# Attention outputs with values as the stationary operand, two heads side by side in the columns

## The chip, the core and the metric

One core of a Trainium2 chip runs the whole program. The metric is device time in microseconds (us). The core's engines are TensorE (PE: matmuls and transposes; PEld in the profile: its weight loads), VectorE (DVE), ScalarE (ACT), GpSimd (POOL) and SyncE (SP, which issues the DMAs). A matmul reads a stationary operand, loaded into the 128 x 128 array first, and streams a moving operand through it.

## The reference

A decoder trunk of two layers over 256 tokens of width 1024, in float32. In each layer the input is RMS-normed and multiplied by one large matrix whose columns feed four token mixers of 4 heads x 64 and four gates. All mixers end in softmax attention:

```python
# A: top-64 keys by an indexer, one shared key/value head
# B: causal over all 256 keys, 4 key/value heads
# C: compressed keys + selected blocks + window, each with sigmoid gates
# D: window 128, 2 key/value heads, learned sinks
p = masked_softmax(q @ k.T * 64 ** -0.5, ok)      # e / max(sum(e), 1e-30)
o = p @ v                                         # (256 tokens, 4 heads, 64)
y = concat(o over heads)                          # (256, 256)
m = sum over mixers of sigmoid(gate) * (y @ w_branch)
x = x + m @ w_out
x = x + down(conv_silu_gate(up(rms_norm(x))))
```

With 256 tokens mixer C runs its "selected" and its "window" attention over all causal keys, each with its own keys and values, and adds both to the compressed one, each part scaled by a gate for each token and head.

## The kernel before

Tokens lie in two blocks of 128 (`NT = 2`), with the token on the partition, or transposed, with the feature on the partition and 256 token columns. Every weight matrix is loaded in chunks (`loads`, line 440), copied to a rounded part by ScalarE (`split_hi`, 460) and subtracted by VectorE to a rest (`split_lo`, 470); three products (rounded activations x rounded weights, rest x rounded, rounded x rest) make up one float32 product (`macs`, 490). These are the records `mm<-hi,ahi`, `mm<-hi,alo`, `mm<-lo,ahi` of the profile (and `ahi,hi` and so on in the feed-forward part).

The order of instructions is worked out while the program is built. Each piece of work is a stream, a generator that yields `(engine, needs, rings)` ahead of what it emits; `Flow.run` (140) always emits the step that can start first by estimated clocks, priorities breaking ties. A step that asks for engine "AV" goes to ScalarE or VectorE (line 149):

```python
eng = "ACT" if max(self.clock["ACT"], t) <= max(self.clock["DVE"], t) + 100 else "DVE"
```

`Eng.cost` (180) holds the estimates. Every engine then executes its instructions in that order. `main` (1246) is the stream of the large products: the projections of mixers A, B, D, C, then for each mixer its gate chunks and `branch_out` (1299), which multiplies y with `w_branch`. The mixers are streams beside it that start as their projections are out.

`attend` (632) is called ten times a layer: once for each block of 128 queries (t = 0, 1) in A, B, D, and twice in C (`nsa`, lines 999 to 1015). A call with t = 0 sees 128 keys, one with t = 1 sees 256. It makes scores over the 64 partitions of a head (line 646; the even heads in the lower half of the partitions, the odd ones in the upper half), masks them and takes the maximum (`attend_max`, 729), exponentiates each head on ScalarE with the sum as a by-product (653), spawns `recip` (708: maximum with 1e-30, reciprocal, in C times the gate), transposes the unnormalized exponentials `Sx` on TensorE (675, 681), copies them out of PSUM as `pT` (`evac_tr`, 739), and multiplies:

```python
for h in range(H):
    for b in range(t + 1):
        te = P.matmul(op[:, h, :], pT[:, h, b, :], vfn(h, b), start=b == 0, stop=b == t)
```

Here `pT[:, h, b, :]` (128 keys x 128 queries) is loaded as the stationary operand and 64 columns of values move. The result has the query on the partition. VectorE multiplies it with the reciprocal `rd` on the way out of PSUM (696 or 700), and in C adds it to y in a second step (703). When a mixer's y (128 x 2 x 256) is complete, `y_T` (579) calls `rows_T` (564): four transposes on TensorE (570), a rounding copy by ScalarE (573) and a subtraction by VectorE (575) give the two parts that `branch_out` needs.

`nsa_cmp` (1056) is C's attention over 15 compressed keys; it handles four heads in one product per block of queries (line 1092) and normalizes on the way out (1096).

Buffers are rings: PSUM banks for large products (`mm_r`, four), scores (`sc_r`, two) and transposes and small products (`tr_r`, two); two buffers for `Sx` (`sx_r`), two for `pT` (`pt_r`), four sets of small statistics (`sm_r`), one temporary `ot_r` (1017).

In the profile a float32 product stands as two load-and-matmul records, a transpose as one. `tr<-slotQ,f` and `tr<-kvA,f` are the products of probabilities (`f`) and values (`slotQ` for B, C, D, `kvA` for A), `tr<-cst,slotQ` the transposes of y, `sc<-qk` the scores. A shape such as "128*128 128x64" means 128 rows by 128 columns loaded and 128 x 64 moved. All calls go through one helper, so every line is given as L212.

Of the kernel before, what the change touches and what calls it, by code (L numbers as in the profile page):

```python
# [32 lines left out]
def constants():  # L33
    """What depends on shapes alone: identity, causal masks, rotary tables, a selection of rows."""
    c = np.zeros((128, C_END), np.float32)
    i = np.arange(128)
    c[:, C_ID:C_TRI] = np.eye(128)
    j = np.arange(256)
    diff = (128 + i)[:, None] - j[None, :]
    c[:, C_TRI:C_DM] = np.where(diff >= 0, 0.0, NEG)  # L40
    c[:, C_DM:C_CM] = np.where((diff >= 0) & (diff < 128), 0.0, NEG)
    t = (np.arange(2)[None, :, None] * 128 + i[:, None, None])
    ok = (np.arange(NCMP) * 16 + 31)[None, None, :] <= t
    c[:, C_CM:C_OK] = np.where(ok, 0.0, NEG).reshape(128, 30)
    c[:, C_OK:C_COS] = ok.reshape(128, 30)
    for dim, a, b in ((64, C_COS, C_SIN), (32, C_COSI, C_SINI)):
        inv = np.float32(10000.0) ** (-np.arange(0, dim, 2, dtype=np.float32) / np.float32(dim))
        ang = np.arange(S, dtype=np.float32)[:, None] * inv[None, :].astype(np.float32)
        co, si = np.cos(ang), np.sin(ang)
        cd = np.concatenate([co, co], 1).reshape(2, 128, dim).transpose(1, 0, 2)  # L50
        sd = np.concatenate([si, -si], 1).reshape(2, 128, dim).transpose(1, 0, 2)
        c[:, a:a + 2 * dim] = cd.reshape(128, 2 * dim)
        c[:, b:b + 2 * dim] = sd.reshape(128, 2 * dim)
    for h in range(H):
        c[32 * h:32 * h + 32, C_BLK + h] = 1.0
    for cc in range(2):
        for n in range(NCMP):
            for v in range(2):
                c[30 * v + 15 * cc + n, C_SEL + 15 * cc + n] = 1.0
    return c  # L60


# [8 lines left out]
class Ring:  # L71
    """slots that streams take and give back"""
# [14 lines left out]
class Flow:  # L87
    """A step of a stream is what it emits after `yield (engine, needs, rings)`: instructions of that
    one engine. The step that can start first is emitted next, so each engine meets its
    instructions in the order in which their operands are expected."""  # L90
# [23 lines left out]
    def moved(self, byts):  # L114
        """a transfer: issued in turn, eight under way at most, one after the other through the engines"""
        s = max(self.clock["SP"], self.need, self.ends[-8] if len(self.ends) >= 8 else 0.0)
        self.emitted = True
        self.clock["SP"] = s + 475
        self.wire = max(self.wire, s + 1100) + byts / 360.0
        self.ends.append(self.wire + 900)  # L120
        return self.ends[-1]
# [52 lines left out]
class Eng:  # L174
    """an engine of nc whose calls also advance the expected clock"""

    def __init__(self, flow, name, real):
        self.flow, self.name, self.real = flow, name, real

    def cost(self, m, a, k):  # L180
        aps = [v for v in list(a) + list(k.values()) if hasattr(v, "shape")]
        n = max(free_size(v) for v in aps)
        psum = any(v.tensor.name[:2] in ("mm", "sc", "tr") and v.tensor.name[2].isdigit() for v in aps)
        if self.name == "PE":
            n = free_size(a[0])
            if m == "transpose":
                c = 0.835 * n
            else:
                c = 0.417 * n + 2 if a[1].dtype == F32R else 1.67 * max(n, free_size(a[1])) + 2
            return c * (1 if self.flow.clock["PE"] > 6700 else 2)  # L190
        ptrs = sum(hasattr(k.get(q), "shape") for q in ("scale", "bias", "accum_out", "scalar"))
        if self.name == "ACT":
            return (52 if psum else 98) + 0.833 * n + 93 * ptrs
        if self.name == "DVE":
            if m == "tensor_copy" and not psum:
                return 62 + 0.54 * n
            if m == "scalar_tensor_tensor":
                ptrs = hasattr(a[2], "shape")
            elif m == "tensor_tensor_reduce":
                ptrs -= 1  # L200
            else:
                ptrs = 0
            return 68 + 1.04 * n + 62 * ptrs
        if self.name == "POOL":
            return 310 + 165 * n if k.get("op") == ALU.pow else 120 + 2.14 * n
        return 50
# [22 lines left out]
def trunk(ctx: ExitStack, tc: tile.TileContext, a, out):  # L229
# [72 lines left out]
    def warm():  # L302
        """the tensor engine's clock rises after some microseconds of work: keeps it busy until the first products"""
# [19 lines left out]
    def rsqrt(o, scale):  # L323
        """after a step of DVE: o = (o * scale + eps) ** -0.5"""
# [165 lines left out]
    def macs(ch, pieces, ps, get, futs, k0, first, last, ends=None):  # L490
        """rows: ps[t] += act(k0..) @ chunk"""
# [72 lines left out]
    def rows_T(src, needs, dst, k0, fut, scale=1.0):  # L564
        """256 columns of rows into two tiles of transposed halves"""
# [13 lines left out]
    def y_T(y, yf, yT, f):  # L579
        yT += yield "PE", [yf], [y_r]  # L580
        yield from rows_T(y, [yf], yT[0], 0, f)

# [7 lines left out]
    def head_rstd(src, h, d, r, rt, needs):  # L590
        """r (128, NT * h) = rsqrt of the mean square of src (128, NT, h, d)"""
# [8 lines left out]
    def rope(o, src, h, d, c, s, rt, needs, dup=1):  # L600
        """src (128, NT, h, d) -> o (128, NT, h, dup, d)"""
# [18 lines left out]
    def T_pairs(o, src, n, needs):  # L620
        """rows (128, NT, n * 128) -> o (128, n, 256)"""
# [10 lines left out]
    def attend(t, qT, kblk, kT, vfn, scl, mask, y, needs, sink=None, fin=None, gate=None):  # L632
# [30 lines left out]
        fl.spawn(recip(t2, den, rd, gate, rdf), 8)  # L663
        tes = []
        pTt = None
        for g in range(t + 1):
            if g == 0:
                pTt, tb = yield "PE", [te], [pt_r, tr_r]
                pT = pTt.rearrange("p (h b q) -> p h b q", h=H, b=2)
            else:  # L670
                tb, = yield "PE", [], [tr_r]
# [14 lines left out]
        sx_r.give(sxt, tq)  # L686
        ob, = yield "PE", tes, [tr_r]
        op = ob[:, :256].rearrange("p (h d) -> p h d", h=H)
        for h in range(H):
            for b in range(t + 1):  # L690
                te = P.matmul(op[:, h, :], pT[:, h, b, :], vfn(h, b), start=b == 0, stop=b == t)
        pt_r.give(pTt, te)
        rdb = rd[:, :, None].to_broadcast([128, H, DH])
        if gate is None:
            yield "DVE", [te, rdf], []
            te = V.tensor_tensor(heads(y)[:, t], op, rdb, op=ALU.mult)
            tr_r.give(ob, te)
        else:
            otmp, = yield "DVE", [te, rdf], [ot_r]
            te = V.tensor_tensor(otmp, op, rdb, op=ALU.mult)  # L700
            tr_r.give(ob, te)
            yield "DVE", [te], []
            te = V.tensor_tensor(heads(y)[:, t], heads(y)[:, t], otmp, op=ALU.add)
            ot_r.give(otmp, te)
        sm_r.give(sm, te)
# [12 lines left out]
    class _Pair(Fut):  # L718
        """known once both entries of a list are"""
# [24 lines left out]
    def qk_done(slot, futs, t_fut, n):  # L744
        """gives the slot back and notes y once n units are through"""
# [271 lines left out]
    ot_r = Ring([junk[:, :256].rearrange("p (h d) -> p h d", h=H)])  # L1017

    class Hidden:
        """what the products with c_cmp_w1 take from and give to the mixer"""  # L1020
# [4 lines left out]
    def hidden(i, ch, hid):  # L1025
        """pairs of chunks side by side: the blocks on the diagonal are wanted"""
# [29 lines left out]
    def nsa_cmp(qT, needs, tvb, cgv, y, y0):  # L1056
        """two heads a product over queries and compressed keys, four over probabilities and compressed values"""
# [25 lines left out]
        fl.spawn(cmp_den(tp_, Pv, crd, cgv, crd_f := Fut()), 12)  # L1083
        pTt, tb = yield "PE", [tp_], [pt_r, tr_r]
# [6 lines left out]
        for t in range(NT):  # L1091
            te = P.matmul(tb[:, t * 256:t * 256 + 256], pTt[:, t * 128:t * 128 + 128], vbd.rearrange("p h d -> p (h d)"),
                          start=True, stop=True)
        pt_r.give(pTt, te)
        yield "DVE", [te, crd_f], []
        te = V.tensor_tensor(heads(y), tb.rearrange("p (t h d) -> p t h d", t=NT, h=H),
                             crd[:, :, :, None].to_broadcast([128, NT, H, DH]), op=ALU.mult)
# [62 lines left out]
    def taps(col, ci_, u, a, z, t, f, fa):  # L1160
        """one channel block: the last tap, with the bias, and the first one into z; the middle one into a"""
# [10 lines left out]
    def conv(col, u, a, z, c0, t):  # L1172
        """two channel blocks through the causal convolution"""
# [8 lines left out]
    def conv_pair(col, ps, rg, g, t, rbf, cs, tmp, gf, gT, f):  # L1182
        """a bank of two channel blocks; the gates also through their silu"""
# [21 lines left out]
    def gated(tmp, needs, cs, gT, f):  # L1205
        """the gates times the values, in two parts"""
# [11 lines left out]
    def conv_first(col, bank, te, rbf, g, tmp, gf, gT, f):  # L1218
        """the first pair, with a bank for each block"""
# [26 lines left out]
    def main():  # L1246
        def open_layer(l, xf):
            """what the products of a layer start from"""
# [11 lines left out]
        for l in range(DEPTH):  # L1260
# [20 lines left out]
            # first group: both chunks over the first half of k, then over the second  # L1281
# [165 lines left out]
```

## Time and profile before

| | us |
|---|---|
| median of 3 runs | 881.3 |
| the runs | 881.3, 881.18, 885.47 |
| span of the profiled execution, first to last instruction | 884.2 |
| the profiled execution's own time | not listed; of the three runs only 885.47 is longer than the span |
| TensorE busy | 877.4 |
| VectorE busy | 675.7 |
| ScalarE busy | 535.8 |

A busy time is the union of an engine's records. Matmul records overlap, as one starts before the one ahead has left the array; what a matmul costs TensorE is read from the distance of starts in the timeline. A timeline row merges neighbours of the same form on an engine: start, time from the first start to the last end, count.

### The profile page before, as it was taken

How to read it: one execution, taken by the hardware profiler on the slowest of the kernel's cores; microseconds unless marked ns; L12 is line 12 of the kernel's file. 1: busy time of each engine (PE TensorE's matmuls, PEld its weight loads, DVE VectorE, ACT ScalarE, POOL GpSimd, SP SyncE). 2: the span in 40 equal slices, each digit the busy share in tenths (PEclk: the TensorE clock that was granted, in tenths of full speed). 3: DMA queues.
4: the chain of work that ended last, by engine and by line, in shares of the span. 5: the costliest groups of instructions: out<-in, count | busy, mean ns of one | idle time of the engine just before them, and what ended most of it. 6: DMA issues, size and time to landing. Idle time of an engine off the chain costs nothing.

```text
span 884.2 us, 14084 instructions
## 1 busy us (share of the span) xinstructions
PE 877.4 (99%) x5435; PEld 770.9 (87%) x5435; DVE 675.7 (76%) x1301; ACT 535.8 (61%) x907; POOL 35.1 (4%) x30
## 2 busy tenths in 40 slices
PE   8999999999999999999999999999999999999998
PEld 8979787788889999998898888887888899999886
DVE  4779988956767999984557998978476599899652
ACT  5555575644557887864455466646454598888531
POOL 0111002000000000000000111010000000000000
PEclk9999999999999999999999999999999999999999
DMA  7727454144645756555555264452446556556560
GB/s 264 237 87 238 143 187 148 48 143 147 215 162 168 229 166 220 184 183 190 160 181 167 78 211 143 143 171 74 161 167 216 165 164 218 191 192 192 173 230 24
DMA packets 103412, 149.89 MB, mean 170 GB/s; under 512 B 4072, under 2 KB 62258, under 8 KB 103346
## 3 DMA queue, kind: packets, MB, share of 16 engines
q1 hardware_dynamic: 103346, 149.01, 52.0%
q8 instruction: 42, 0.69, 0.3%
q14 instruction: 24, 0.20, 0.1%
HBM read 147.95 MB, written 1.05 MB: 169 GB/s over the span
## 4 chain that ended last, share of the span: by engine, by line
PE 98%; DMA 1%; ACT 0%; SPq 0%; DVE 0%; issue 0%; DVEq 0%
PE mm L212 82%; PE tr L212 8%; PE sc L212 8%; DMA rn<-in_norm_g_dram 1%; ACT f L212 0%; ACT L212 0%; SPq L239 0%; ACT hi L212 0%; DVE x L212 0%; DVEq L1443 0%
## 5 line engine op out<-in xcount | busy, mean ns | idle before, releaser
L212 DVE TENSOR_TENSOR lo<-raw,hi 128x1024 fp32r<-128x1024 f32 (+3 forms) x288 | 337.7, 1179 | 119.9 <-ACT hi L212 112.7
L212 ACT ACTIVATE hi<-raw 128x1024 fp32r<-128x1024 f32 (+3 forms) x288 | 291.5, 1023 | 167.8 <-PE mm L212 145.6
L212 PE MATMUL mm<-hi,ahi 128*128 128x512 f32 (+4 forms) x480 | 178.0, 377 | 0.0
L212 PE MATMUL mm<-hi,alo 128*128 128x512 f32 (+4 forms) x480 | 172.4, 365 | 0.0
L212 PE MATMUL mm<-ahi,hi 128*128 128x256 f32 x640 | 152.4, 279 | 0.0
L212 PE MATMUL mm<-alo,hi 128*128 128x256 f32 x640 | 152.1, 278 | 0.0
L212 PEld LDWEIGHTS mm<-ahi,hi 128*128 128x128 f32 x640 | 120.6, 188 | 0.1
L212 PEld LDWEIGHTS mm<-alo,hi 128*128 128x128 f32 x640 | 120.5, 188 | 0.1
L212 PE MATMUL mm<-lo,ahi 128*128 128x512 f32 (+4 forms) x480 | 118.2, 369 | 0.0
L212 PEld LDWEIGHTS mm<-hi,ahi 128*128 128x128 f32 x480 | 90.8, 189 | 15.3 <-issue 3.0
L212 PEld LDWEIGHTS mm<-hi,alo 128*128 128x128 f32 x480 | 90.8, 189 | 11.3
L212 PEld LDWEIGHTS mm<-lo,ahi 128*128 128x128 f32 x480 | 83.0, 188 | 14.2 <-issue 2.0
L212 PE MATMUL mm<-hi,slotQ 128*128 128x512 f32 x352 | 88.9, 392 | 0.0
L212 PE MATMUL mm<-ahi,lo 128*128 128x256 f32 x640 | 88.2, 278 | 0.0
L212 PEld LDWEIGHTS mm<-ahi,lo 128*128 128x128 f32 x640 | 80.4, 188 | 0.0
L212 PEld LDWEIGHTS mm<-hi,slotQ 128*128 128x128 f32 x352 | 66.0, 188 | 14.5
L212 ACT ACTIVATE f<-f,col 128x256 f32<-128x256 f32 x88 | 48.1, 594 | 14.5 <-DVE f L212 14.0
L212 PE MATMUL mm<-lo,slotQ 128*128 128x512 f32 x176 | 48.3, 393 | 0.0
L212 PE MATMUL sc<-qk 64*128 64x128 f32 (+3 forms) x224 | 40.4, 348 | 0.0
L212 ACT ACTIVATE slotP<-mm,rh 128x512 f32<-128x512 f32 x32 | 20.3, 684 | 31.3 <-PE mm L212 31.2
L212 ACT ACTIVATE qk<-f,col 128x256 f32<-128x256 f32 x88 | 39.2, 495 | 0.0
L212 PEld LDWEIGHTS mm<-lo,slotQ 128*128 128x128 f32 x176 | 32.9, 188 | 7.1
(222 smaller groups left out, 1099.5 us busy)
## 6 DMA issues: line engine op xcount, KB each, us to landing
raw<-in_w_up_dram SPq DMA_DIRECT2D x44, 1024.0 KB, 5.1
raw<-in_w_in_dram SPq DMA_DIRECT2D x40, 1024.0 KB, 5.0
raw<-in_w_down_dram SPq DMA_DIRECT2D x20, 1024.0 KB, 5.0
raw<-in_w_out_dram SPq DMA_DIRECT2D x8, 1024.0 KB, 5.1
raw<-in_w_branch_dram SPq DMA_DIRECT2D x6, 1024.0 KB, 5.7
raw<-in_w_in_dram SPq DMA_DIRECT2D x7, 768.0 KB, 6.5
raw<-in_w_in_dram SPq DMA_DIRECT2D x4, 592.0 KB, 4.2
raw<-in_w_in_dram SPq DMA_DIRECT2D x4, 536.0 KB
```

Source lines behind the costliest of these rows:

```text
L212: fn(*a, **k)
```

## The change

- `y` now holds the transposed output (head parity and feature on the partition, head pair, token): no transposes in `y_T`, whose copy and subtraction now read SBUF.
- In `attend` the exponentials of each head are multiplied with `rd` before they are transposed, on ScalarE or VectorE. The transposes of the first two heads (t = 1) or of all four (t = 0) wait for it.
- The products load the values (128 keys x 64) and move `pT` (128 queries); even heads write PSUM partitions 0 to 63, odd heads 64 to 127. The planner's cost is halved there (`P.side = 2`).
- The result leaves PSUM by a copy on either engine, or in C by one addition into y; `ot_r` goes, and `sm_r` is given back after the scaling.
- `nsa_cmp` normalizes ahead of its transposes and loads the values.
- Docstrings and comments go.

```diff
@@ Eng.__init__, Eng.cost
+        self.side = 1
-            return c * (1 if self.flow.clock["PE"] > 6700 else 2)
+            return c / self.side * (1 if self.flow.clock["PE"] > 6700 else 2)
@@ y_T
-        yT += yield "PE", [yf], [y_r]
-        yield from rows_T(y, [yf], yT[0], 0, f)
+        yT += yield "ACT", [yf], [y_r]
+        te = A.activation(yT[0][0], y, AF.Copy)
+        yield "DVE", [te], []
+        f.t = V.tensor_tensor(yT[0][1], y, yT[0][0].bitcast(F32), op=ALU.subtract)
@@ attend
         fl.spawn(recip(t2, den, rd, gate, rdf), 8)
+        tn = []
+        for h in range(H):
+            eng, _ = yield "AV", [rdf], []
+            if eng == "ACT":
+                tn.append(A.activation(Sx[:, h, :nk], Sx[:, h, :nk], AF.Copy, scale=rd[:, h:h + 1]))
+            else:
+                tn.append(V.tensor_scalar(Sx[:, h, :nk], Sx[:, h, :nk], rd[:, h:h + 1], None, op0=ALU.mult))
...
-                pTt, tb = yield "PE", [te], [pt_r, tr_r]
+                pTt, tb = yield "PE", tn if t == 0 else tn[:2], [pt_r, tr_r]
...
-                tb, = yield "PE", [], [tr_r]
+                tb, = yield "PE", tn[2:], [tr_r]
...
         sx_r.give(sxt, tq)
+        sm_r.give(sm, max(tn))
+
         ob, = yield "PE", tes, [tr_r]
-        op = ob[:, :256].rearrange("p (h d) -> p h d", h=H)
-        for h in range(H):
+        op = ob[:, :256].rearrange("p (k q) -> p k q", k=2)
+        P.side = 2
+        for k in range(2):
             for b in range(t + 1):
-                te = P.matmul(op[:, h, :], pT[:, h, b, :], vfn(h, b), start=b == 0, stop=b == t)
+                for par in range(2):
+                    te = P.matmul(op[64 * par:64 * par + 64, k, :], vfn(2 * k + par, b), pT[:, 2 * k + par, b, :],
+                                  start=b == 0, stop=b == t)
+        P.side = 1
         pt_r.give(pTt, te)
-        rdb = rd[:, :, None].to_broadcast([128, H, DH])
+        yt = y[:, :, t * 128:t * 128 + 128]
         if gate is None:
-            yield "DVE", [te, rdf], []
-            te = V.tensor_tensor(heads(y)[:, t], op, rdb, op=ALU.mult)
-            tr_r.give(ob, te)
+            eng, _ = yield "AV", [te], []
+            te = copy_on(eng, yt, op)
         else:
-            otmp, = yield "DVE", [te, rdf], [ot_r]
-            te = V.tensor_tensor(otmp, op, rdb, op=ALU.mult)
-            tr_r.give(ob, te)
             yield "DVE", [te], []
-            te = V.tensor_tensor(heads(y)[:, t], heads(y)[:, t], otmp, op=ALU.add)
-            ot_r.give(otmp, te)
-        sm_r.give(sm, te)
+            te = V.tensor_tensor(yt, yt, op, op=ALU.add)
+        tr_r.give(ob, te)
         fin(te)
@@ nsa_cmp
+        yield "DVE", [tp_, crd_f], []
+        tp_ = V.tensor_tensor(Pv, Pv, crd[:, :, :, None].to_broadcast([128, NT, H, 15]), op=ALU.mult)
...
-        for t in range(NT):
-            te = P.matmul(tb[:, t * 256:t * 256 + 256], pTt[:, t * 128:t * 128 + 128], vbd.rearrange("p h d -> p (h d)"),
-                          start=True, stop=True)
+        for k in range(2):
+            te = P.matmul(tb[:, k * 256:k * 256 + 256], vbd[:, 2 * k:2 * k + 2, :], pTt[:, 0:256], start=True, stop=True)
...
-        yield "DVE", [te, crd_f], []
-        te = V.tensor_tensor(heads(y), tb.rearrange("p (t h d) -> p t h d", t=NT, h=H),
-                             crd[:, :, :, None].to_broadcast([128, NT, H, DH]), op=ALU.mult)
+        eng, _ = yield "AV", [te], []
+        te = copy_on(eng, y, tb.rearrange("p (k q) -> p k q", k=2))
```

## Rows read from the trace of the kernel before

**Rows 1.** The page: busy time of each engine; the chain that ended last

```profile
PE 877.4 (99%) x5435; PEld 770.9 (87%) x5435; DVE 675.7 (76%) x1301; ACT 535.8 (61%) x907; POOL 35.1 (4%) x30
...
PE 98%; DMA 1%; ACT 0%; SPq 0%; DVE 0%; issue 0%; DVEq 0%
```

**Rows 2.** The view of waits, TensorE: who waited for what, us in total, times, longest

```profile
PE sc L212 <- DMA rn<-in_norm_g_dram: 1.8, 1, 1.8
```

**Rows 3.** Groups by shape, TensorE: names, shapes, count | busy us, mean ns | idle before

```profile
L212 PE MATMUL tr<-slotQ,f 128*128 128x64 f32 x192 | 23.7, 273 | 0.0
...
L212 PE MATMUL tr<-kvA,f 128*128 128x64 f32 x48 | 5.9, 272 | 0.0
...
L212 PE MATMUL tr<-cst,slotQ 128*128 128x128 f32 x36 | 5.6, 272 | 0.0
```

**Rows 4.** Timeline, TensorE matmuls: start us, us, line, operation, count

```profile
98.42 1.89 PE L212 MATMUL tr<-kvA,f 128*128 128x64 f32 x16
...
121.45 1.00 PE L212 MATMUL tr<-slotQ,f 128*128 128x64 f32 x8
122.28 0.61 PE L212 MATMUL tr<-cst,f 128*128 128x128 f32 x4
...
189.37 1.08 PE L212 MATMUL mm<-lo,ahi 128*128 128x512 f32 x4
190.29 1.89 PE L212 MATMUL tr<-slotQ,f 128*128 128x64 f32 x16
191.99 0.48 PE L212 MATMUL mm<-hi,ahi 128*128 128x512 f32 x1
192.31 0.39 PE L212 MATMUL mm<-hi,alo 128*128 128x512 f32 x1
```

**Rows 5.** Timeline, TensorE weight loads of one block of 16

```profile
98.20 1.98 PEld L212 LDWEIGHTS tr<-kvA,f 128*128 128x128 f32 x16
```

**Rows 6.** Timeline, TensorE: transposes of a finished output and what follows

```profile
208.67 0.60 PE L212 MATMUL tr<-cst,slotQ 128*128 128x128 f32 x4
209.03 0.48 PE L212 MATMUL mm<-hi,ahi 128*128 128x512 f32 x1
209.34 0.40 PE L212 MATMUL mm<-hi,alo 128*128 128x512 f32 x1
```

**Rows 7.** Timeline, TensorE: score blocks over 32 and over 64 rows

```profile
51.51 0.71 PE L212 MATMUL sc<-qk 32*128 32x128 f32 x4
52.14 0.50 PE L212 MATMUL mm<-hi,ahi 128*128 128x512 f32 x1
...
82.25 0.39 PE L212 MATMUL mm<-hi,ahi 128*128 128x512 f32 x1
82.47 0.40 PE L212 MATMUL mm<-hi,alo 128*128 128x512 f32 x1
82.80 0.72 PE L212 MATMUL sc<-qk 64*128 64x128 f32 x8
83.45 0.73 PE L212 MATMUL mm<-lo,ahi 128*128 128x512 f32 x2
```

**Rows 8.** Timeline, TensorE: small products ahead of the first weights

```profile
7.03 0.56 PE L212 MATMUL sc<-f 128*64 128x64 f32 x6
```

**Rows 9.** Groups by shape, VectorE: names, shapes, count | busy us, mean ns

```profile
L212 DVE TENSOR_TENSOR slotQ<-tr,rd 128x256 f32<-128x256 f32 x12 | 5.1, 422 | 8.0 <-PE tr L212 7.6 <-ACT cg L212 0.3
...
L212 DVE TENSOR_SCALAR sel<-acc 128x256 f32<-128x256 f32 x2 | 0.6, 288 | 0.0
...
L212 DVE TENSOR_SCALAR sel<-acc 128x128 f32<-128x128 f32 x2 | 0.4, 224 | 0.0
```

**Rows 10.** Busy time in two stretches: PE, PEld, DVE, ACT, POOL; clock, DMA, GB/s

```profile
60.00:120.00 60.00, 60.00 (x354) 50.97 (x353) 56.14 (x158) 37.13 (x76) 5.44 (x2) 1.00 0.52 163
120.00:200.00 80.00, 80.00 (x445) 65.21 (x445) 62.03 (x181) 44.56 (x99) 5.44 (x3) 1.00 0.39 128
```

More of the change, by code (lines that the diff above doesn't have):

```diff
@@ L1015, in nsa @@
                                 fin=fin, gate=cgv[:, t, :, 1 + i]), 13 + 2 * i + t)
-    ot_r = Ring([junk[:, :256].rearrange("p (h d) -> p h d", h=H)])
     class Hidden:
```

## The prediction

> **What bounds the kernel now.** I read the page first. TensorE is busy for 877.4 of 884.2 us, and 98% of the chain that ended last is TensorE's own work [rows 1]; VectorE is busy 76% and ScalarE 61%. The view of waits then asks whether TensorE is ever kept waiting: the longest entry is 1.8 us, for a load before the first product [rows 2]. So the time is the sum of what TensorE issues, and a part of the change is worth what it takes from that sum, as long as the other engines keep up.
>
> The list of groups by shape says what the change touches. The products of probabilities and values stand there as 192 + 48 records of 128 x 64, two records for each product in the code (10 attention calls a layer: five of 4 products, five of 8; two layers). The transposes of finished outputs are 32 of the 36 records of the third row [rows 3] (the other 4 are the latents of mixer A). A busy time or a mean of such rows is not what a record costs, since ends overlap with the next start; the timeline gives the distance between starts. A block of 8 records takes from 121.45 to 122.28, 0.83 us, and a block of 16 from 190.29 to 191.99, 1.70 us: 0.104 and 0.106 each. Weight products follow each other at 0.92 / 4 = 0.23 us (189.37 to 190.29), but the first after a block takes 0.32 (191.99 to 192.31), so where one follows, as after about half of the blocks, 0.09 more belongs to the block [rows 4]. I take 0.87 for the block of 8 and 1.75 for the block of 16: 10 x 0.87 + 10 x 1.75 = 26.2 us for the twenty blocks.
>
> Why 0.105 us for 64 moving columns? The weight loads of a block of 16 run from 98.20 for 1.98 us, 0.12 each, side by side with the matmuls [rows 5]. Loading 128 columns of probabilities sets the pace, not the 64 columns that pass.
>
> **The change part by part.**
>
> *Transposes of y, removed.* Four transposes start at 208.67 and the next weight product at 209.03; that product takes 0.31 to the following start, 0.08 over the usual 0.23 [rows 6]. So 0.36 + 0.08 = 0.44 us a block, 8 blocks: **-3.5 us**, on the path. The ScalarE copy and the VectorE subtraction after them stay, at the same 128x512, and now read SBUF; both lie beside TensorE.
>
> *The products, turned round.* The same 240 records remain. Now 64 columns of values are loaded and 128 columns of probabilities pass, and two heads go to columns 0 to 63 and 64 to 127 of the array. The trace has no two column halves at work, but it has the same thing by rows: scores use 64 rows, and the two parities of heads lie in different halves. Eight score records with 128 moving columns take from 82.80 to 83.45, 0.65 us, while four index scores of the same 128 columns that had no partner (51.51 to 52.14) take 0.63 [rows 7]. So partners run at the same time. The block costs more than it lasts: the product before it takes 0.33 instead of 0.23 (82.47 to 82.80), and the two behind it 0.73 less the last one's own 0.39, 0.34 instead of 0.23. So entering and leaving cost 0.65 + 0.10 + 0.11 = 0.86 us for four paired steps. A step of 128 moving columns is 0.11 (half of a 512-column product's 0.23 for its two passes over them), so 0.86 - 0.44 = 0.42 is the price of the switch, first load included. With loads half as wide, I take off 0.06 (half of the 0.12 of rows 5): **0.36**. That narrow loads are cheap is seen at the start, where six records of 64 x 64 take 0.56 us, tail included [rows 8].
>
> After: block of 8, 4 x 0.11 + 0.36 = 0.80; block of 16, 8 x 0.11 + 0.36 = 1.24; together 10 x 2.04 = 20.4. **-5.8 us**, on the path. Ends: with no switch cost at all, 13.2 us (-13.0); with the rows' full 0.42, 21.6 (-4.6); with no pairing, a rival, below. I take the value near the upper end, since a switch is seen at every score block.
>
> Here the Trainium skill has a rule against the change: its page "TensorE: Matmul & The Clock Gate", section "Part 3: Packing small matmuls", says that a weight load overlaps a running matmul only when the row groups differ, and both column halves use all rows. Rows 5 show loads of all 128 rows running beside matmuls of the same rows, which disagrees; what it would do here is the third rival.
>
> *Normalizing probabilities, added.* Four new steps a call, 80 in all, each over 128x128 or 128x256, on whichever of ScalarE and VectorE the planner's clock frees first. Nearest rows are VectorE's scalings of these shapes in SBUF: 0.288 and 0.224 us [rows 9]. All on VectorE that is 40 x 0.288 + 40 x 0.224 = 20.5 us. Removed from VectorE: 20 multiplications of 0.422, -8.4; 12 copies replace multiplications on either engine, at most +5.1; the gated addition is only moved. So VectorE's load changes by -8.4 to +17 us over two layers, and ScalarE takes the rest. Cost on the path: **0**. The cover: in 60 to 200 us VectorE idles 140 - 56.14 - 62.03 = 21.8 us and ScalarE 140 - 37.13 - 44.56 = 58.3 us, while TensorE never stops [rows 10]. If the cover is gone, see the second rival.
>
> *Waits.* The transposes of probabilities used to wait for the exponentials and now also for the reciprocal chain and two or four scalings: three small steps, none above 0.224, plus two of 0.288, some 1.3 us longer a call as an estimate from rows 9. Behind a waiting transpose stand other streams' products: the planner orders TensorE's queue by expected start, and weight products fill it. The scaled rows leave their buffer later, and there are only two, so up to five pairs of calls a layer could shift by 1.3 us each, 6.5 us at the last. That is covered: mixer D's last products end at 191.99 and its output is first needed at 208.67, 16.7 us later [rows 4, 6]. Bounds: 0 and, were none covered, 2 x 6.5 = 13 us.
>
> *The compressed branch.* As many records, the same 256 moving columns and 128 loaded; one small VectorE multiplication more, one turned into a copy. 0. No transfer is added or moved, so SP's queue keeps its issues; POOL keeps its powers. Buffers of the small statistics come back earlier, the temporary of the gated sum goes: 0.
>
> *Order.* Every changed duration reshuffles the planner's order, and score blocks pair up or not by it: two unpaired blocks of four cost about 0.8 us more than one paired block of eight [rows 7]. Four pairings won or lost are 3.2 us, either way; I take 0.
>
> Sum: -3.5 - 5.8 = -9.3 us. The profile's span is 884.2; of the three runs (881.18, 881.3, 885.47) only the slowest is long enough to hold it, so the profiled execution lies some 1.3 us over its span and about 4 over the median. Saved work doesn't depend on that: 881.3 - 9.3 = **872.0 us**.
>
> **The rivals.**
>
> 1. *The halves don't run side by side*, so the change doesn't do what it says. Then a block of 8 takes 8 x 0.11 + 0.36 = 1.24 and one of 16 takes 2.12: 33.6 us, +7.4; with -3.5, **885.2**. For it: no row shows column pairs. Against: row pairs work, also with two passes a product. Chance 0.12.
>
> 2. *Normalizing makes VectorE the bound*, the mechanism that ends slower: it stands at the transposes of probabilities and the split of weights behind it, in the stretches where VectorE is already full. With all scalings and copies there, +17 us of VectorE work, all exposed: 872.0 + 17 = **889**. It decides once more than 9.3 of the 17 us are exposed. For it: VectorE is busy 56.14 of 60 us in 60 to 120. Against: the idle time above, and that the planner gives a step to VectorE only if ScalarE is later by over 0.1 us (line 149). Chance 0.09.
>
> 3. *Loads are exposed in column mode.* A step becomes 0.11 + 0.06 = 0.17: 0.36 + 4 x 0.17 = 1.04 and 1.72, together 27.6, +1.4; with -3.5, **879.2**. For it: nothing in the trace. Against: rows 5, and six records of rows 8 in 0.56 us, where loads of 0.06 and matmuls of 0.06 in turn would need 0.72. It is the rule cited above. Chance 0.05.
>
> **How the numbers follow.** The forecast has 0.72, and 0.02 is left for what I don't see. Its own span is 866 (switch half as dear, -3.6, and three pairings won, -2.4) to 877 (nothing saved by narrow loads and four pairings lost, +4.4, rounded up). The range is 866 to 881.5: it takes in the third rival, and part of the second, and leaves out the first, whose 0.12 with the far end of the second is within the 2 in 10. Half a per cent (4.4 us) is what a measurement of this kernel can tell from none. Faster: 0.66 of the forecast, 0.01 of the rest, 0.67. Same: most of rivals 1 and 3 and a share of 2, 0.22. Slower: 0.11.
>
> **What would show it.** Right: no transposes of y; output products starting in pairs some 0.01 us apart, at 0.11 per pair, with a first start about 0.1 late on entering and on leaving; TensorE still 99% busy; scalings mostly on ScalarE. Wrong: output records 0.11 apart one by one (rival 1), 0.17 (rival 3), or idle TensorE ahead of transposes or weight products with VectorE named as releaser (rival 2). A count of paired score blocks far from before would show that the order, not the change, moved the time.

## The result and the profile after

The change is slower by half a per cent: 886.97 us (median of 11 runs, 884.02 to 890.4) against 881.3 (11 runs, 880.45 to 886.09), ratio 1.0052 [1.0033, 1.0071]. By the ratio that is +4.6 us (the medians lie 5.7 apart) where -9.3 was forecast, so 13.9 us are missing. One of the four runs of e3 below took 946.1 us at a granted clock of 0.85 and is left out of its ratio, though not of its median.

The profiled executions can't be set against each other by their spans (884.2 before, 883.0 after; the latter took 884.66 in all). The 320 records `mm<-ahi,hi` of the first layer's up-projection, not touched by the change, take 124.3 us from the first start to the last in one and 120.3 in the other, with the clock at 1.00 in both; the windows below show 509 against 529 records in 60 us. Other kernels of this study show the one or the other (e1 and e4 below 124.4, e3 and e5 120.3). So I compare by stage: from a layer's first weight product to its last product with y, read from the starts in the timeline. Layer 1 went from 228.4 to 233.0 us, layer 2 stayed at 226.3. The sum, +4.6, is what the ratio says too; apart from the up-projection and a start that is 1.6 us earlier in the profile of after (first weight product at 7.3 instead of 8.9) the other stages agree within 0.1 us.

The page of the kernel after: busy times, the granted clock in 40 slices, and the chain that ended last; these answer to [rows 1].

```profile
PE 866.3 (98%) x5403; PEld 751.6 (85%) x5403; DVE 679.1 (77%) x1314; ACT 557.0 (63%) x968; POOL 35.0 (4%) x30
...
PEclk9999979999999999999999999899999999999999
...
PE 94%; DVE 2%; DMA 2%; ACT 0%; SPq 0%; issue 0%; DVEq 0%; ACTq 0%
```

TensorE's busy time fell by 11.1 us, 4 of them from the pace of the up-projection, and its share of the chain fell from 98 to 94%: work was saved, and standing still took its place. The clock, 9s before, has a 7 in the slice from 110 us and an 8 in that from 552. The view of waits of the kernel after (what waited for what, us in total, times, longest) names them; before there was nothing of the kind behind the start [rows 2].

```profile
PE tr L213 <- DVE qr L213: 2.8, 1, 2.8
PE sc L213 <- DVE mx L213: 2.3, 2, 2.1
PE mm L213 <- DVE yhi L213: 2.0, 1, 2.0
```

Gaps of TensorE over 0.1 us add up to 12.7 us, against 2.8 before; behind the first weight product they are 11.6 against none. The groups by shape of the kernel after, with the scalings on both engines and the products that answer to [rows 3] (busy us, mean ns, idle before):

```profile
L213 ACT ACTIVATE f<-f,rd 128x256 f32<-128x256 f32 x29 | 13.0, 500 | 1.6 <-DVE rd L213 1.6
L213 ACT ACTIVATE f<-f,rd 128x128 f32<-128x128 f32 x28 | 9.3, 392 | 3.3 <-DVE rd L213 2.9 <-DVE den L213 0.4
...
L213 DVE TENSOR_SCALAR f<-f,rd 128x256 f32<-128x256 f32 x11 | 3.4, 349 | 0.1
L213 DVE TENSOR_SCALAR f<-f,rd 128x128 f32<-128x128 f32 x12 | 2.8, 278 | 0.0
...
L213 PE MATMUL tr<-f,slotQ 128*64 128x128 f32 x192 | 14.5, 287 | 0.2 <-DVE f L213 0.2
...
L213 PE MATMUL tr<-cst,slotQ 128*128 128x128 f32 x4 | 0.8, 272 | 0.0
```

57 of the 80 scalings went to ScalarE. They took 0.392 and 0.500 us there and 0.278 and 0.349 on VectorE, where the prediction had 0.224 and 0.288 from other steps of these shapes. The transposes of y are gone (36 records before, 4 left, those of A's latents).

**Where TensorE stands still.** The timeline of the kernel after, rows of PE, PEld, ACT and DVE (start, us, engine, operation, count, and in brackets the idle time before it and what ended that):

```profile
94.93 0.40 PE L213 MATMUL mm<-hi,alo 128*128 128x512 f32 x1
95.25 0.66 PE L213 MATMUL tr<-f,kvA 128*64 128x128 f32 x8
95.84 0.50 PE L213 MATMUL mm<-hi,ahi 128*128 128x512 f32 x1
96.18 0.39 PE L213 MATMUL mm<-hi,alo 128*128 128x512 f32 x1
...
101.04 1.09 PE L213 MATMUL tr<-f,kvA 128*64 128x128 f32 x16
101.04 0.85 PEld L213 LDWEIGHTS tr<-f,kvA 128*64 128x64 f32 x16 [0.17 <-issue]
102.07 1.19 PE L213 MATMUL mm<-lo,ahi 128*128 128x512 f32 x4
...
101.63 0.85 ACT L213 ACTIVATE rt<-slotQ 128x768 f32<-128x768 f32 x1
...
106.95 1.20 PE L213 MATMUL mm<-lo,ahi 128*128 128x512 f32 x4
110.95 0.66 PE L213 MATMUL tr<-cst,qr 128*128 128x128 f32 x4 [2.80 <-DVE qr L213]
...
116.31 0.49 DVE L213 TENSOR_TENSOR rt<-slotQ,cst 128x128 f32<-128x128 f32 x2
...
124.78 0.40 DVE L213 TENSOR_TENSOR ylo<-kr,ylo 128x240 fp32r<-128x240 f32 x1
...
124.92 0.73 PE L213 MATMUL mm<-hi,yhi 128*60 128x256 f32 x4 [2.02 <-DVE yhi L213]
125.45 1.05 PE L213 MATMUL mm<-lo,yhi 128*60 128x256 f32 x4
...
129.41 0.61 PE L213 MATMUL tr<-cst,kn 60*128 60x15 f32 x4
```

The same stretch of the kernel before:

```profile
100.75 0.48 DVE L212 TENSOR_TENSOR rt<-slotQ,cst 128x128 f32<-128x128 f32 x2
...
110.21 0.40 DVE L212 TENSOR_TENSOR ylo<-kr,ylo 128x240 fp32r<-128x240 f32 x1
...
111.25 0.63 PE L212 MATMUL mm<-hi,yhi 128*60 128x256 f32 x4
...
114.15 0.61 PE L212 MATMUL tr<-cst,kn 60*128 60x15 f32 x4
...
144.20 0.85 ACT L212 ACTIVATE rt<-slotQ 128x768 f32<-128x768 f32 x1
```

The same place in the second layer, first before, then after:

```profile
553.81 0.40 DVE L212 TENSOR_TENSOR ylo<-kr,ylo 128x240 fp32r<-128x240 f32 x1
...
557.02 0.63 PE L212 MATMUL mm<-hi,yhi 128*60 128x256 f32 x4
...
559.92 0.61 PE L212 MATMUL tr<-cst,kn 60*128 60x15 f32 x4
```

```profile
544.66 1.18 PE L213 MATMUL mm<-lo,ahi 128*128 128x512 f32 x4
...
556.09 2.07 PE L213 MATMUL sc<-qk 64*128 64x256 f32 x4 [2.13 <-DVE mx L213]
558.09 1.11 PE L213 MATMUL mm<-hi,yhi 128*60 128x256 f32 x4
...
562.93 0.61 PE L213 MATMUL tr<-cst,kn 60*128 60x15 f32 x4
```

The records of 60 loaded columns are C's products with its compression weights (`hidden`, line 1025). `main` executes them at a fixed place in its stream, behind the gate products of A. Their inputs `yhi` and `ylo` are made by C's stream. Before, the last of them was done at 110.21 + 0.40 = 110.61 and the products started at 111.25 with no idle time: 0.6 us to spare. Now `ylo` is done at 125.18 and `yhi`, the one waited for, just before the products start at 124.92, and `main`, that is, every weight product, stands behind it: between 108.15 and 124.92 only pieces of the mixers run. In the second layer it is the same from 545.84 (544.66 + 1.18) to 558.09, but there the last input is done at 557.14, 0.95 us ahead of the start: what stands in front of `hidden` in TensorE's queue is a score block, which waited 2.13 us for a maximum.

C is late because of a buffer. The four mixers share one set of temporaries (`prep_r`, line 258). D asks for it on ScalarE (line 886), C on VectorE (910), and the planner gives it to the one that can start first, priorities breaking ties only. The first instruction that writes it tells who had it: in C a VectorE product of 128x128, in D a ScalarE square of 128x768. Before, C had it at 100.75 and D at 144.20; after, D has it at 101.63 and C at 116.31, 15.6 us later than before. In the second layer D is first in both, so the change did not turn the order there; C starts 4.1 us later (550.87 after, 546.81 before).

The windows of the kernel after (us, then busy time of PE, PEld, DVE, ACT, POOL, the granted clock, DMA share, GB/s):

```profile
108.00:111.00 3.00, 0.20 (x2) 0.05 (x1) 2.98 (x12) 3.00 (x11) 0.56 (x1) 1.00 0.00 0
...
113.00:115.00 2.00, 1.72 (x7) 1.29 (x8) 1.97 (x8) 1.94 (x5) 0.00 (x0) 0.50 0.00 0
...
123.00:125.00 2.00, 0.09 (x1) 0.09 (x2) 1.97 (x8) 1.33 (x3) 0.00 (x0) 1.00 0.03 8
...
127.00:129.00 2.00, 2.00 (x12) 2.00 (x11) 0.95 (x6) 2.00 (x7) 1.03 (x1) 0.55 0.00 0
...
108.15:124.92 16.77, 10.29 (x66) 7.38 (x65) 14.40 (x53) 13.84 (x44) 0.41 (x1) 0.80 0.18 64
545.84:558.09 12.25, 8.45 (x57) 5.27 (x57) 11.99 (x37) 6.96 (x16) 0.00 (x0) 0.89 0.35 125
...
265.00:325.00 60.00, 60.00 (x529) 59.82 (x528) 54.61 (x83) 48.93 (x80) 0.69 (x1) 1.00 0.58 186
```

And one of the kernel before, for the up-projection:

```profile
260.00:320.00 60.00, 60.00 (x509) 59.53 (x508) 52.69 (x81) 47.38 (x76) 0.70 (x1) 1.00 0.58 181
```

Standing still costs twice. TensorE was busy for 0.20 of 3 us from 108 on, and from 113 to 115 its clock was at the lower of its two levels (1.2 instead of 2.4 GHz); after 0.09 of 2 us from 123 on it was so for most of 127 to 129. So the first 24 records of `hidden` take 4.49 us (124.92 to 129.41) where they took 2.90 (111.25 to 114.15), and 4.84 (558.09 to 562.93) instead of 2.90 (557.02 to 559.92) in layer 2. Idle time behind the first weight product, 11.6, and these two, 1.6 + 1.9, make 15.1 us; three pairs of score blocks that the order won (the table below) give back some 2.4. So about 12.7 of the 13.9 missing us are accounted for, and the rest is not.

### The profile page after: what moved, and what is told of

It reads as the page before. It is cut to its first block, busy times and chain, and to the rows that moved or that the text cites. A ratio compares the mean times of both kernels' runs of the same rounds, so it can differ in the third digit from the quotient of the medians.

```text
span 883.0 us, 14092 instructions
## 1 busy us (share of the span) xinstructions
PE 866.3 (98%) x5403; PEld 751.6 (85%) x5403; DVE 679.1 (77%) x1314; ACT 557.0 (63%) x968; POOL 35.0 (4%) x30
## 4 chain that ended last, share of the span: by engine, by line
PE 94%; DVE 2%; DMA 2%; ACT 0%; SPq 0%; issue 0%; DVEq 0%; ACTq 0%
PE mm L213 80%; PE sc L213 8%; PE tr L213 6%; DMA raw<-in_w_in_dram 2%; DMA x<-in_x_dram 1%; DVE f L213 1%; DVE kr L213 0%; SPq L240 0%; DVE kn L213 0%; DVE rt L213 0%; DVE lo L213 0%; ACT hi L213 0%; ACT f L213 0%; DVE qk L213 0%; DVE alo L213 0%
## 5 line engine op out<-in xcount | busy, mean ns | idle before, releaser
L213 PE MATMUL mm<-ahi,hi 128*128 128x256 f32 x640 | 150.0, 277 | 0.0
L213 PE MATMUL mm<-alo,hi 128*128 128x256 f32 x640 | 149.7, 276 | 0.0
L213 ACT ACTIVATE f<-f,nmx 128x128 f32<-128x128 f32 (+1 forms) x80 | 35.4, 445 | 9.4 <-DVE nmx L213 9.3
```

What stands on the lines that cost most here:

```text
L213: fn(*a, **k)
```

## The experiments

Two theories. *Order*: the change itself gains about what was forecast, and loses it because D takes the temporaries first. *Scalings*: normalizing ahead of the transposes holds up the transposes and the engines, and the order is only a symptom. Each kernel is compared with runs of the kernel before on the same chip. "Layer 1" and "layer 2" are the two stages defined above, in one profiled execution; the last column counts the score blocks of heads over 64 rows in which eight records ran in pairs, and those of four without a partner. The runs of the kernel before lie near 881 or near 885 us, about as far apart as the two paces of the up-projection put them, so smaller differences than that are read by stage.

| kernel | ratio to before | layer 1 | layer 2 | scores 8 / 4 |
|---|---|---|---|---|
| before | 1 | 228.4 | 226.3 | 12 / 16 |
| after | 1.0052 [1.0033, 1.0071] | 233.0 | 226.3 | 15 / 10 |
| e1: after, C first | 0.9940 [0.9916, 0.9963] | 226.8 | 221.9 | 10 / 20 |
| e2: after without scalings, D first | 0.9906 [0.988, 0.9933] | 229.5 | 220.8 | 14 / 12 |
| e3: after without scalings, C first | 0.9833 [0.9803, 0.9862] | 223.0 | 221.0 | 14 / 12 |
| e4: before, D first | 1.0087 [1.0059, 1.0116] | 236.6 | 226.3 | 14 / 12 |
| e5: before with scalings | 1.0015 [0.9991, 1.0039] | 230.3 | 226.3 | 12 / 16 |
| e6: before, C first | 1.0011 [0.9989, 1.0032] | 229.2 | 226.5 | 12 / 16 |
| e7: after, C first, scalings unawaited | 0.9907 [0.987, 0.9944] | 227.2 | 221.5 | 9 / 22 |
| e10: after, C first, scalings on VectorE | 0.9911 [0.989, 0.9933] | 225.0 | 219.2 | 14 / 12 |
| e8: after, C first, scores paired | 0.9848 [0.9807, 0.9889] | 224.3 | 217.8 | 20 / 0 |
| e9: before, scores paired | 0.9917 [0.99, 0.9933] | 225.7 | 222.9 | 20 / 0 |

**e1: the new kernel with C first.** One wait in the planner, none on the chip: D's stream may ask for the temporaries once C has them. In layer 1 that is the order of the kernel before; in layer 2, where D was first before too, it is a new one.

```diff
+    c_got = [Fut() for _ in range(DEPTH)]
@@ swa (D)
-        (prep,) = yield "ACT", [pf, tab_f[l]], [prep_r]
+        (prep,) = yield "ACT", [pf, tab_f[l], c_got[l]], [prep_r]
@@ nsa (C)
         (prep,) = yield "DVE", [pf, tab_f[l]], [prep_r]
+        c_got[l].t = 0.0
```

> The changed kernel, with one edit: mixer D may take the shared set of temporaries only after mixer C has. Order theory: in the changed kernel TensorE stood still at 106 to 125 us and at 546 to 558 us, ahead of the products with C's compressed weights, because D took the temporaries first; with C first those waits (some 11 us of idle time, and some 4 us of slower clock behind them) mostly go and the kernel takes 870 to 875, 0.988 to 0.993 of before. Latency theory: the scalings ahead of the transposes keep TensorE waiting whatever the order; then the idle time stays near 10 us and the time is 882 to 887.

Measured: 878.74 us (6 runs), 0.9940, just above the 0.988 to 0.993 of the order theory; against the change as it was, -6.2 us in layer 1 and -4.4 in layer 2. The timeline of e1, first at `hidden`, then at a score block:

```profile
110.16 0.68 PE L213 MATMUL mm<-hi,yhi 128*60 128x256 f32 x4 [1.73 <-DVE yhi L213]
110.68 0.63 PE L213 MATMUL mm<-lo,yhi 128*60 128x256 f32 x4
111.14 0.62 PE L213 MATMUL mm<-hi,yhi 128*60 128x256 f32 x4
...
171.44 0.71 PE L213 MATMUL sc<-qk 64*128 64x128 f32 x4
172.08 0.66 PE L213 MATMUL tr<-f,slotQ 128*64 128x128 f32 x8
```

The 15 us delay of layer 1 is gone and the sign of the result has turned, by an edit that changes no computation. 1.7 us of idle time stay ahead of `hidden`, and more score blocks have lost their partners: the block of four here takes 0.64 where one of eight takes 0.65 [rows 7].

**e4: the old kernel with the new order.** The same wait the other way round, in the kernel before.

```diff
+    d_got = [Fut() for _ in range(DEPTH)]
@@ swa (D)
         (prep,) = yield "ACT", [pf, tab_f[l]], [prep_r]
+        d_got[l].t = 0.0
@@ nsa (C)
-        (prep,) = yield "DVE", [pf, tab_f[l]], [prep_r]
+        (prep,) = yield "DVE", [pf, tab_f[l], d_got[l]], [prep_r]
```

> The kernel before, with D held ahead of C in both layers (before, only the second layer had it so). Order theory: TensorE gets idle time ahead of C's compressed products in the first layer too, 3 to 10 us, so 884 to 891. Latency theory: the order alone costs little, within 2 us of before, 880 to 883.

Measured: 893.72 us (5 runs), 1.0087, as the order theory had it when its 884 to 891 are set against 881.3; +8.2 us in layer 1, nothing in layer 2, where D was first already. Its windows show the same place and the same double cost, idle time and then the low clock:

```profile
110.00:115.00 5.00, 3.05 (x24) 2.47 (x24) 4.48 (x17) 4.38 (x12) 0.00 (x0) 1.00 0.01 5
...
120.00:125.00 5.00, 3.90 (x11) 2.48 (x10) 4.92 (x19) 1.33 (x3) 0.00 (x0) 0.50 0.25 97
```

None of the change's own edits is in this kernel, so in layer 1 the order alone suffices for a loss of this size.

**e2 and e3: without the scalings.** The exponentials go to the transposes unscaled (so these two leave the normalization out); e2 holds D first, e3 C first.

```diff
-        tn = []
-        for h in range(H):
...
+        tn = [te] * H
...
-        sm_r.give(sm, max(tn))
+        sm_r.give(sm, te)
```

> The changed kernel without the scaling of the probabilities in attend (its outputs stay unnormalized there), D held ahead of C in both layers as in the changed kernel. Order theory: the waits ahead of C's compressed products stay in good part, idle time of TensorE 5 us or more, 876 to 884. Latency theory: without the scalings the chain is as short as before, idle time under 2 us, 868 to 873.

> The changed kernel without the scaling of the probabilities in attend (outputs unnormalized there), C ahead of D in both layers. Both theories: no long idle time on TensorE, so this is what the products and the missing transposes of y are worth alone: 866 to 872. What it lies below the run with scalings and C first is the price of the scalings: 1 to 4 us by the order theory, 12 or more by the latency theory.

Measured: e2 875.98, e3 870.01 us (before: 885.41 in this set). The time of e2 alone does not decide: set against before it lies at the edge of the other theory's range. Its idle time does, 6.6 us behind the first weight product where that theory had under 2. With after and e1 these make a square, layer by layer:

| | layer 1, D first | C first | layer 2, D first | C first |
|---|---|---|---|---|
| with scalings | 233.0 | 226.8 | 226.3 | 221.9 |
| without | 229.5 | 223.0 | 220.8 | 221.0 |

In layer 1 the order costs 6.2 us with and 6.5 without scalings, and the scalings 3.5 to 3.8 in either order: two separate prices. In layer 2, D first costs nothing without scalings and 4.4 with them. There the kernel before had 2.8 us between the last input of `hidden` (done at 554.21) and its start (557.02); that only both together use up this room fits the square and is not shown in another way. From e3 to after that is 15.3 us, and how it divides depends on what is counted first: 10.6 for the order and 4.7 for the scalings by way of e1, 6.3 for the order and 9.0 for the scalings by way of e2. The order that the change itself turned is that of layer 1, 6.2 to 6.5 us. So neither theory holds alone, and by the square the scalings are not free: 4.7 us with C first, where 1 to 4 or 12 and more were expected.

**e5 and e6: the scalings in the old kernel.** e5 adds them ahead of the transposes and turns the scaling on the way out into a copy or an addition, with the products as they were. C happened to take the temporaries first in both layers, so e6, the kernel before with e1's wait, is its partner.

```diff
+            eng, _ = yield "AV", [rdf], []
+            if eng == "ACT":
+                tn.append(A.activation(Sx[:, h, :nk], Sx[:, h, :nk], AF.Copy, scale=rd[:, h:h + 1]))
...
-            te = V.tensor_tensor(heads(y)[:, t], op, rdb, op=ALU.mult)
-            tr_r.give(ob, te)
+            te = copy_on(eng, heads(y)[:, t], op)
```

> The kernel before, with the four scalings of a call moved ahead of the transposes of the probabilities and a plain copy or addition behind the products; products and transposes of y stay as before (C comes ahead of D in both layers here). This is the price of the scalings alone, against the run of the kernel before with C first. If they are hidden beside TensorE: within 2 us of that run. If their latency or load reaches TensorE: 4 to 9 us above it.

> The kernel before, with C held ahead of D in both layers (before, only in the first). Order theory: the second layer had no idle time on TensorE with D first, so nothing is to be won there: within 2 us of before, ratio 0.998 to 1.002. If C first is better in itself: 3 us or more faster.

Measured: e5 886.49, e6 885.45 us (10 runs each, before 885.09): 1.0015 and 1.0011, neither to be told from 1 or from each other. By stages e5 is 0.9 us over e6. In the old kernel the scalings were hidden, as the prediction had it; that the new one hides them less because its TensorE has some 10 us less to do is a guess that no run tests.

**e7: nobody waits for the scalings.** e1, with the same number of operations of the same shapes reading a constant and writing a scratch area; transposes wait for the exponentials alone (normalization is left out).

```diff
-                tn.append(A.activation(Sx[:, h, :nk], Sx[:, h, :nk], AF.Copy, scale=rd[:, h:h + 1]))
+                A.activation(scr_a[:, :nk], tri[:, :nk], AF.Copy, scale=mhalf[:, 0:1])
...
+        tn = [te] * H
```

> The changed kernel with C first; the scalings keep their number, shapes, engines and places in the order, but work on a constant and a scratch buffer, so nothing waits for them (outputs unnormalized in attend). If the scalings cost by their load on VectorE and ScalarE: as the run with scalings and C first, 0.992 to 0.996 of before. If they cost by the wait of the transposes: as the run without scalings and C first, 0.982 to 0.986.

Measured: 875.32 us, 0.9907. By medians that lies between e1 and e3, with an interval that overlaps e1's. But the profiled e1 has the slow pace of the up-projection (124.4) and the profiled e7 the fast one (120.3); the two layers together take 448.7 us in both. By stages, then, taking the wait away won nothing. But e7 is not e1 in all else: it has one pair of score blocks fewer (some 0.8 us), 2.84 us of idle time ahead of `hidden` instead of 1.73, and the lower clock behind it, which e1 does not have in these layers:

```profile
111.00:114.00 3.00, 3.00 (x15) 3.00 (x16) 3.00 (x12) 1.02 (x3) 0.00 (x0) 0.50 0.03 3
```

These could hide some 3 us that the wait does cost. One execution of each does not settle whether the price of the scalings is the wait or what 80 more operations do to the order.

**e10: all 80 scalings on VectorE.** e1, with the choice of the engine taken away.

```diff
-            eng, _ = yield "AV", [rdf], []
+            yield "DVE", [rdf], []
+            eng = "DVE"
```

> The changed kernel with C first and all 80 scalings on VectorE (of the changed kernel's, 57 are on ScalarE). It tests the second rival of the prediction: if VectorE's load is what the scalings cost, TensorE idles or waits more and the time rises by 4 us or more over the run with C first, 0.998 to 1.006 of before. If it is not, 0.988 to 0.996 as with C first, or a little better, since a scaling takes 0.28 and 0.35 us there instead of 0.39 and 0.50.

Measured: 877.9 us, 0.9911, no slower than e1 and 4.5 us faster by stages. Busy times on its page:

```profile
PE 864.6 (99%) x5403; PEld 751.1 (86%) x5403; DVE 683.7 (78%) x1361; ACT 541.7 (62%) x921; POOL 33.4 (4%) x30
```

VectorE carries all the scalings and is still only 78% busy: over the whole kernel it is not what the time hangs on. What moved is again the order: 12 score blocks without a partner, as in e3, instead of e1's 20. Four pairs more at about 0.8 us [rows 7] are 3.2 of the 4.5 us. And the two layers together take 444.2 us, where e3, without any scalings, takes 444.0 (2.0 more in layer 1, 1.8 less in layer 2): 4.7 us is the price of the scalings in e1's order, not a price they have in every order. The wait ahead of `hidden` is longer than in e1, and here no low clock follows it; the timeline and a window:

```profile
110.70 0.68 PE L213 MATMUL mm<-hi,yhi 128*60 128x256 f32 x4 [2.69 <-DVE yhi L213]
```

```profile
111.00:113.00 2.00, 2.00 (x20) 2.00 (x18) 2.00 (x8) 1.51 (x4) 0.88 (x1) 1.00 0.00 0
```

**e8 and e9: score blocks that always pair.** e8 is e1, e9 the kernel before; both banks for the scores of a call are asked for in one step, so that nothing can come between the even and the odd heads.

```diff
-                sxt, sm, sc = yield "PE", needs, [sx_r, sm_r, sc_r]
+                sxt, sm, sc, sc1 = yield "PE", needs, [sx_r, sm_r, sc_r, sc_r]
...
-                sc, = yield "PE", [], [sc_r]
+                sc = sc1
```

> The changed kernel with C first, and each call takes both score banks at once, so that its two score blocks always run as a pair of row halves. With C first alone 20 of its score blocks ran without a partner, 10 pairs; each pairing should save about 0.8 us of TensorE: 6 to 8 us below the run with C first, 0.984 to 0.988 of before. If waiting for two free banks costs as much: no gain, 0.992 to 0.996.

> The kernel before, in which each call takes both score banks at once. It tells how much of the gain of the paired-score run belongs to the change: the kernel before has 16 score blocks without a partner, 8 pairs of some 0.8 us. If pairing is worth the same without the change: 5 to 7 us, 0.992 to 0.995 of before. If the wait for two banks eats it: 0.998 to 1.002.

Measured: e8 871.28 us (4 runs, 867.62 to 874.48), 0.9848, faster than both kernels; e9 878.41 (4 runs), 0.9917, just under the 0.992 to 0.995 expected. By stages e8 is 6.6 us under e1 and e9 6.1 under before. In e8 ten pairs are won back, about 8 us, and the wait ahead of `hidden` grows from 1.7 to 2.8, as its view of waits shows:

```profile
PE mm L213 <- DVE yhi L213: 2.8, 1, 2.8
PE mm L213 <- DVE ylo L213: 1.3, 2, 0.7
```

So in layer 1, where this wait lies, e8 wins 2.5 us over e1, and 4.1 in layer 2. The second line is the subtraction in `y_T`: two weight products wait 0.65 us each for it, which none did in after. Pairing is worth about as much without the change as with it; set against e9, the change itself is worth 6.5 us (448.6 - 442.1).

## Why the prediction was wrong

- *Transposes of y*: right. 32 of 36 records are gone, and the copy and the subtraction left in their place are named in no wait of TensorE in after (in e8, with less for TensorE to do, the subtraction is).
- *The products, turned round*: right in mechanism and size. A block of 8 takes 95.84 - 95.25 = 0.59 to the next start; the product before it takes 0.32 and the one behind 0.34 instead of 0.23, together 0.79 (0.80 forecast). A block of 16 takes 1.03 and, with the same 0.20 around it, 1.23 (1.24). So rival 1 falls. Rival 3 falls too: behind the first, pairs of a block start 0.109 us apart, where it needed 0.17, and 16 loads of 64 columns, 0.85 us, run beside the matmuls. The Trainium skill's rule (page "TensorE: Matmul & The Clock Gate", section "Part 3: Packing small matmuls"), by which these loads would be exposed because both halves use all rows, does not agree with this trace.
- The gain of the two together is seen in e3, where neither scalings nor the new order lie over it: 454.7 - 444.0 = 10.7 us by stages. Two pairs of score blocks more than before account for 1.6; 9.1 is left for the 9.3 of the sum. So close a match is in part luck, since e3 also has 1.9 us of idle time that before has not.
- ***Waits* is the step that failed.** It said: "That is covered: mixer D's last products end at 191.99 and its output is first needed at 208.67, 16.7 us later". I looked for the deadline at the end of the mixers, where `main` takes y. The deadline that counted lies in the middle: `main` also takes C's inputs of `hidden`, at a fixed place, and there the kernel before had 0.6 us to spare in layer 1 and 2.8 in layer 2, not 16.7; in layer 1 the last input came 14.6 us later (125.18 for 110.61). What made it late there is in the main the next point; whether the 1.3 us a call of this step had a part stays open (e7). It could have been read in its trace by asking, for each operand that `main` takes from another stream, when it was made and when it was used.
- *Order*: also too narrow. I saw that changed durations reshuffle the planner's order, and priced only the pairing of scores (3.2 us either way). The pairings were won, in fact (10 blocks without a partner instead of 16, some 2.4 us). The price lay in who gets a shared buffer first: 6.2 to 6.5 us in layer 1, where the change turned that order, and 4.4 in layer 2 once the scalings are there. That the wait of e1 alone puts C first again in layer 1 is shown; which estimate of the planner tipped it is not, since no trace holds its clocks.
- *Normalizing*: cost 0 was right for the old kernel (e5) and wrong for the new one: 4.7 us with C first (e1), 9.0 with D first (after against e2), yet 0.2 in e10's order. Rival 2's sign is there: the three longest waits of TensorE, listed above, all name VectorE, which is busy for 14.40 of 16.77 us and 11.99 of 12.25 in the two stretches where TensorE stands. Its mechanism is not: only one scaling in each of these stretches runs on VectorE (0.28 and 0.35 us), its load over the kernel rose by 3.4 us and not 17, and with all scalings on it the time fell (e10). Whether the wait for the scalings costs anything is open (e7). e1 has four pairs of scores fewer than e3, 3.2 us, and 1.7 us of idle time ahead of `hidden`, together 4.9. The outcome was on the slower side for a reason that none of the rivals named.

## What to carry to other kernels

Where a planner or a fixed stream sets the order, how late a part may be is read not at its output alone but at every point where the main stream takes something from it; the smallest room of these, here 0.6 us, is what counts. A change that only shortens steps can hand a shared buffer to another user, so look who takes it first before and after, and hold that order fixed when the change itself is to be judged: with it held, this change is worth 5 us (e1). With the score blocks kept in pairs as well the kernel is 13 us faster than before (e8), but 7 of these the pairs give without the change (e9).

## What the runs showed of the hardware

- Column halves work side by side with float32, which takes two records a product: the two matmuls of a pair start 5 to 7 ns apart, the second pair 0.160 us behind the first and the others 0.109 apart, and weight products around a block lose 0.20 us (0.09 ahead, 0.11 behind).
- Idle stretches of 2.80 and 2.02 us were followed by work at the lower clock: a step of `hidden` took 0.213 us (125.45 to 126.30 for four) instead of 0.117. In e1, behind 1.73 us, the same steps took 0.115 (110.68 to 111.14). The length of one stretch does not tell which it will be: in e10 the clock stayed at 1.00 behind 2.69 us at the same place, in e7 it was 0.50 behind 2.84, and in e4 it was 0.50 from 120 to 125 though no gap was longer than 1.1 us. Of the 15.1 us lost above, idle time shows 11.6; the rest is in no wait.
- The same stream of weight products has two steady paces at a granted clock of 1.00, 0.118 and 0.113 us a record in the windows above (60 us over 509 and 529 records, nearly all of 256 columns). It is not one pace an execution: before has the slower one in its first layer alone (124.3 us, then 119.8), e10 in its second (120.8, then 124.3). No run here shows why.
